# A two-block network on one core: the MLP norms' statistics earlier, one projection's weight split without GpSimd, the last root on ScalarE

## The chip, the cores and the metric

The kernel runs on one core of a Trainium2 chip (trn2). The metric is the device time of one execution in microseconds; lower is better. The median of three runs before the change is 824.85 us.

## The reference

Input is one sequence of 256 tokens with 1024 features; everything is float32. Three residual layers follow one another: a convolution and attention mixer with an MLP (layer 0), a gated recurrence with an MLP (layer 1), and a last block with two attentions over the tokens and a context (block 2).

```python
def rmsnorm(x, g):
    y = x * rsqrt(mean(x * x, -1) + 1e-6)
    return y * g

def first_block(x, ...):
    x = x + mixer_ab(rmsnorm(x, mix_norm[0]), ...)                    # layer 0
    x = x + square(relu(rmsnorm(x, mlp_norm[0]) @ w_up[0])) @ w_down[0]
    u = rmsnorm(x, mix_norm[1]) @ c_w_in                              # layer 1
    gate, xr = split(u, 2)
    y = rg_lru(causal_depthwise_conv(xr, conv_w) + conv_b) * gelu(gate)
    x = x + y @ c_w_out                                               # "layer 1's projection"
    x = x + square(relu(rmsnorm(x, mlp_norm[1]) @ w_up[1])) @ w_down[1]
    return rmsnorm(x, final_norm)

# second_block: h = rmsnorm(x)*(1+scale)+shift, hc the same of the context; MLA and neighborhood
# attention, two gated output products, y @ w_out, residual, and a last rmsnorm
```

## The kernel before

**Layout.** Activations are transposed: 128 features on the partitions, 8 feature blocks of 256 tokens. A matmul multiplies a 128x128 weight block by 256 columns. To keep float32 precision each operand is split into a high and a low part, and each product takes three matmuls (`mm3`, lines 383 to 385): high x high, high weight x low input, low weight x high input. The weights arrive as 240 units of 512 KB in the order of use, by DMA into a ring of 4 buffers (`raw`). `prep` (lines 321 to 326) makes of a unit `wh` (a rounding copy, line 323 on ScalarE) and `wl` (raw minus `wh`, line 326 on VectorE or GpSimd); POLICY names the engines for each unit, as "ag": copy by ScalarE and subtraction by GpSimd, "av": ScalarE and VectorE. The ring of `wh` and `wl` holds 6 units, 12 while `wx` is open, and 14 in a part of it. `more(n)` prepares n units ahead; `unit` takes the next.

**Order.** A list scheduler gives each engine its order when the program is built, from the order in the code and from what is ready in its own model of time; on the chip each engine keeps that order and waits on semaphores. `inorder(engines)` chains what is traced inside it on the named engines in the order of the code; `issue_after(i)` queues instructions behind i on i's own engine alone.

**Statistics.** `ssq` (line 437) squares x on ScalarE in four pieces (line 442) and adds them on GpSimd (lines 444 and 445), into a tile `ssum` of which there is one for each pool. `csum` (line 452) sums over partitions with tiny matmuls into PSUM, `meaneps` (line 458) makes mean + eps on VectorE, `rsq` (line 463) raises to -0.5 on GpSimd, `across` (line 470) broadcasts over partitions with four matmuls, and `spread` (line 476) copies that to SBUF on ScalarE.

**The MLP** (`mlp`, line 972 on). Each of 16 pairs p does `up(p)`, two units of 24 matmuls, then relu and square (`mr`, `mah` on ScalarE, `ma` on GpSimd, `mal` on VectorE); from p = 2 on, two units of the down product follow (`krow`, 24 matmuls each). The norm's factor is applied to the sum at the end: since relu and square are homogeneous, the factor is 1/(mean + eps), the tile `R2`, first read in `proj_tail`. `ssq` stands behind up(4), csum, meaneps and a reciprocal of 128x2 behind up(6), spread behind up(8). `unit` also calls one small background task (`tick`): in MLP 0 the modulation products on VectorE, in MLP 1 the context's statistics (`ctx_setup`). These use the same tile `ssum`: their ssq is the task of the 9th unit, their csum that of the 14th (the second of up(4)), their spread that of the 15th.

**Layer 1's projection** (end of `layer1`). PE and ScalarE are chained in the code's order here. `root(1)` takes a square root on ScalarE and runs four scans on VectorE; `gelu`; `done(p)` multiplies on VectorE and splits the product (ScalarE copy, VectorE subtraction) into the projection's inputs 2p and 2p+1; `wrow(k)` multiplies input k by weight unit `wo1` k. Units 0 to 3 of `wo1` are "ag". The last three rows are in `proj_tail`.

**The end** (`b2_out`). Squares of the result are summed by `stat` (line 1580); meaneps, rsq on GpSimd and across give the last factor; five VectorE multiplications (line 1614) each start a DMA to the output.

Of the kernel before, what the change touches and what calls it, by code (L numbers as in the profile page):

```python
# [11 lines left out]
F32 = mybir.dt.float32  # L12
# [35 lines left out]
POLICY["wo1"] = ("ag",) * 4 + ("av",) * 4  # L48
# [201 lines left out]
class Kern:  # L250
# [183 lines left out]
    def lo(self, l, src, h):  # L434
        self.nc.vector.tensor_tensor(l, src, h.bitcast(F32), op=ALU.subtract)  # L435
# [49 lines left out]
    def run(self):  # L485
# [13 lines left out]
        with self.pool("xp") as xp:  # L499
# [9 lines left out]
            self.pad(cp, 32)  # L509
# [339 lines left out]
    def proj_tail(self, acc, name, ins, gname, g0, xs, R2=None, mp=None, sums=(), after=None):  # L849
# [8 lines left out]
        for b in range(4):  # L858
# [17 lines left out]
            if xs is not None:  # L876
                for k in ks:
                    V.scalar_tensor_tensor(xs[1][:, k], x[:, k], g[k % 2], xs[0][:, k].bitcast(F32),  # L878
                                           op0=ALU.mult, op1=ALU.subtract)
# [91 lines left out]
    def mlp(self, mp, l):  # L971
# [22 lines left out]
        for p in range(16):  # L994
            if l == 0 and p >= 9:
                if p == 9:
                    self.pad(self.cp, 96)
                    self.hs = [self.t(self.cp, [128, 2112], f"hc{c}", F32R) for c in "hl"]
                    self.pad(self.cp, 160)
                self.ahead = min(2 * p - 14, 13)  # L1000
            if l == 1 and p == 4:
                self.wx, self.slot = None, 0
            up(p)
            if p == 4:
                parts = self.ssq(mp, x)
            if p == 6:
                v = self.meaneps(self.csum(parts), D)
                rv = self.t(self.cp, [128, 2], "rv")
                V.reciprocal(rv, v)
            if p == 8:  # L1010
                R2 = self.spread(mp, rv, "R2")
            if p >= 2:
                for k in (2 * p - 4, 2 * p - 3):
                    self.krow(acc, self.unit("down"), A.pop(k), k == 0, False)
# [8 lines left out]
    def layer1(self, lp):  # L1023
# [101 lines left out]
        with self.inorder(*PIN):  # L1125
# [39 lines left out]
            for k in range(4):  # L1165
                if k == 2:
                    done(2)
                if k == 3:
                    done(3)
                wrow(k)  # L1170
                self.more(1 if k == 0 else 2)
# [93 lines left out]
    def b2_kv(self, bp, ep, d):  # L1265
# [96 lines left out]
        zpair("za", 1, ep, cqn)  # L1362
        d.update(kb=kb, vb=vb, krh=krh, krl=krl, ck=ck, wk=wk, va=va, bp=bp)
# [10 lines left out]
    def b2_attn(self, bp, ap, d):  # L1374
# [117 lines left out]
        def gdone(nm, p):  # L1492
            def f(ps):
                tg[nm, p] = self.t(bp, [128, 512], f"t{nm}", bufs=2)
                S.activation(tg[nm, p], ps, AF.Tanh, scale=0.5)
            return f
# [45 lines left out]
    def b2_out(self, op, d):  # L1542
# [11 lines left out]
        for p in range(4):  # L1554
            if p > 1:
                d["gpair"]("ga", p)
                d["gpair"]("gb", p)
                d["oproj"]("oa", p)
            d["oproj"]("ob", p)
            y = tg["ga", p]  # L1560
            V.tensor_tensor(y, y, tg["gb", p], op=ALU.add)
            self.split(self.pair(y), ys[0][:, 2 * p:2 * p + 2], ys[1][:, 2 * p:2 * p + 2])
            if p == 1:
                R1 = self.spread(op, d["r1"], "R1")
                for k in range(8):
                    V.scalar_tensor_tensor(x[:, k], x[:, k], self.p("fin", k), R1, op0=ALU.mult, op1=ALU.mult)
        def orow(w, k, ms, end):
            for m in ms:
                o = last[:, :T] if m == 7 else acc[m // 2][:, (m % 2) * T:(m % 2 + 1) * T]
                c = slice(m * 128, m * 128 + 128)  # L1570
                self.mm3(o, (w[0][:, c], w[1][:, c]), yrow(k), k == 0 and (m % 2 == 0 or m == 7), end)
        for k in range(6):
            orow(self.unit("wo2"), k, range(8), False)
# [8 lines left out]
        def scale(b):  # L1582
            for k in (2 * b, 2 * b + 1):
                S.activation(x[:, k], x[:, k], AF.Copy, scale=self.p("fg2", k))
# [18 lines left out]
        with self.tc.issue_after(si.ins):  # L1603
            for b in range(1, 4):
                scale(b)
# [5 lines left out]
        RF = self.across(self.rsq(self.meaneps(st[:, :2], D)))  # L1611
# [25 lines left out]
```

## Time and profile before

| | us |
|---|---|
| runs: median (lowest to highest) | 824.85 (819.03 to 830.13) |
| the profiled execution | 821.14 |
| its span, first to last instruction | 819.4 |
| PE (TensorE matmuls) busy | 787.9 (96%) |
| DVE (VectorE) busy | 576.4 (70%) |
| ACT (ScalarE) busy | 473.2 (58%) |
| POOL (GpSimd) busy | 199.0 (24%) |

The profiled execution lies 3.71 us under the median. All times in the views are from the start of the span. PE counts as busy while any matmul is in its pipeline, so a stretch without idle time can still differ in how many matmuls start in it; the windows view gives that number behind an x. PEclk is the granted clock as a share of 2.4 GHz. A line such as L326 is that of the helper which issued the instruction.

### The profile page before, as it was taken

What the parts mean: (1) busy time and instruction counts of PE and PEld (TensorE: products, weight loads), DVE (VectorE), ACT (ScalarE), POOL (GpSimd) and SP (SyncE); (2) the same over time, 40 slices, a digit from 0 to 9 for tenths busy, and PEclk for the clock granted to TensorE, in tenths of its full rate; (3) what the DMA queues carried; (4) which work ended last, traced back from release to release, by engine and by line L of the source; (5) the groups of instructions that cost most, each with busy time, mean ns of one, the idle gap of its engine ahead of it and who ended that gap; (6) DMA issues with size and microseconds to landing.
All of it is one profiled execution on the core that took longest, in us unless ns stands there. A gap on an engine that the chain in (4) does not pass through costs nothing.

```text
span 819.4 us, 16154 instructions
## 1 busy us (share of the span) xinstructions
PE 787.9 (96%) x6480; PEld 756.0 (92%) x6480; DVE 576.4 (70%) x952; ACT 473.2 (58%) x739; POOL 199.0 (24%) x151
## 2 busy tenths in 40 slices
PE   6999989999999999979999999999999999999996
PEld 5997889999999999978999999999989988889996
DVE  6999669999989787578746545557634877565843
ACT  5568656455545657877745444445626587765533
POOL 4796643011101202330531110111000022320001
PEclk9999999999999999999999999999999999999997
DMA  7874357787988832238726656664335533555531
GB/s 239 292 222 130 103 181 247 292 311 272 322 307 283 286 113 88 62 124 302 239 99 210 193 189 190 197 196 164 94 119 151 159 105 102 176 163 176 185 101 52
DMA packets 41259, 152.32 MB, mean 186 GB/s; under 512 B 4576, under 2 KB 5088, under 8 KB 39008
## 3 DMA queue, kind: packets, MB, share of 16 engines
q1 hardware_dynamic: 40752, 149.19, 55.5%
q10 hardware_dynamic: 432, 2.10, 0.7%
q8 instruction: 51, 0.84, 0.4%
q14 instruction: 24, 0.20, 0.1%
HBM read 149.17 MB, written 2.10 MB: 185 GB/s over the span
## 4 chain that ended last, share of the span: by engine, by line
PE 59%; issue 19%; DVE 8%; ACT 8%; POOL 4%; DMA 2%; SPq 0%; POOLq 0%; DVEq 0%; ACTq 0%
PE mm L383 10%; PE mm L384 10%; PE mm L385 10%; PE acc L384 7%; PE acc L383 7%; PE acc L385 7%; POOL ma L989 3%; PE acc L1423 2%; PE acc L1451 2%; PE mm L1460 2%; ACT wh L323 1%; DMA raw<-in_wst 1%; DVE wl L326 1%; PE mm L470 1%; DMA x<-in_xT 1%
## 5 line engine op out<-in xcount | busy, mean ns | idle before, releaser
L323 ACT ACTIVATE wh<-raw 128x1024 fp32r<-128x1024 f32 (+1 forms) x190 | 198.3, 1048 | 162.5 <-PE mm L384 64.2
L326 DVE TENSOR_TENSOR wl<-raw,wh 128x1024 fp32r<-128x1024 f32 (+1 forms) x159 | 197.6, 1250 | 100.1 <-ACT wh L323 98.3
L383 PE MATMUL mm<-xsh,wh 128*128 128x256 f32 x752 | 210.4, 280 | 0.0
L384 PE MATMUL mm<-xsl,wh 128*128 128x256 f32 x752 | 209.1, 278 | 0.0
L385 PE MATMUL mm<-xsh,wl 128*128 128x256 f32 x752 | 209.1, 278 | 0.0
L383 PEld LDWEIGHTS mm<-xsh,wh 128*128 128x128 f32 x752 | 141.7, 188 | 3.7 <-issue 3.3
L384 PEld LDWEIGHTS mm<-xsl,wh 128*128 128x128 f32 x752 | 141.7, 188 | 0.6 <-DVE xsl L878 0.2
L385 PEld LDWEIGHTS mm<-xsh,wl 128*128 128x128 f32 x752 | 141.3, 188 | 0.0
L989 POOL TENSOR_TENSOR ma<-mr 128x512 f32<-128x512 f32 x32 | 49.5, 1548 | 246.2 <-ACT mr L987 246.2
L384 PE MATMUL acc<-mal,wh 128*128 128x256 f32 x360 | 100.1, 278 | 1.0 <-DVE mal L435 1.0
L383 PE MATMUL acc<-mah,wh 128*128 128x256 f32 x360 | 100.3, 279 | 0.0
L385 PE MATMUL acc<-mah,wl 128*128 128x256 f32 x360 | 100.0, 278 | 0.0
L326 POOL TENSOR_TENSOR wl<-raw,wh 128x1024 fp32r<-128x1024 f32 x31 | 74.2, 2414 | 43.8 <-ACT wh L323 43.8
L323 ACT ACTIVATE wxh<-raw 128x1024 fp32r<-128x1024 f32 x47 | 49.2, 1055 | 38.8 <-DMA raw<-in_wst 34.9
L384 PEld LDWEIGHTS acc<-mal,wh 128*128 128x128 f32 x360 | 67.9, 189 | 1.2 <-DVE mal L435 1.2
L383 PEld LDWEIGHTS acc<-mah,wh 128*128 128x128 f32 x360 | 67.7, 188 | 0.0
L385 PEld LDWEIGHTS acc<-mah,wl 128*128 128x128 f32 x360 | 67.6, 188 | 0.0
L326 DVE TENSOR_TENSOR wxl<-raw,wxh 128x1024 fp32r<-128x1024 f32 x44 | 56.6, 1299 | 8.0 <-ACT wxh L323 8.0
L384 PE MATMUL mm<-xsl,wxh 128*128 128x256 f32 x208 | 58.1, 279 | 0.6 <-DVE xsl L878 0.6
L383 PE MATMUL mm<-xsh,wxh 128*128 128x256 f32 x208 | 58.3, 280 | 0.0
L385 PE MATMUL mm<-xsh,wxl 128*128 128x256 f32 x208 | 58.0, 279 | 0.0
L915 DVE CUSTOM_DVE_ANT_0 mdump<-mw,cv 128x1024 f32<-128x1024 f32 x40 | 48.7, 1217 | 2.7 <-DMA mw<-in_modw 2.6
(386 smaller groups left out, 1855.9 us busy)
## 6 DMA issues: line engine op xcount, KB each, us to landing
raw<-in_wst SPq DMA_DIRECT2D x240, 512.0 KB, 4.1
mw<-in_modw SPq DMA_DIRECT2D x12, 1024.0 KB, 7.2
nb<-in_nab SPq DMA_DIRECT2D x16, 256.0 KB, 3.7
ab<-in_alibi ACTq DMA_DIRECT2D x1, 1536.0 KB, 8.9
x<-in_xT SPq DMA_DIRECT2D x4, 256.0 KB, 4.9
cv<-in_cvec SPq DMA_DIRECT2D x1, 1024.0 KB, 4.7
cx<-in_cT SPq DMA_DIRECT2D x1, 1024.0 KB, 7.3
xd<-x SPq DMA_DIRECT2D x1, 1024.0 KB, 4.6
```

What stands on the lines that cost most here:

```text
L323: nc.scalar.activation(wh, r, AF.Copy)
L326: (nc.vector if lo == "v" else nc.gpsimd).tensor_tensor(wl, r, wh.bitcast(F32), op=ALU.subtract)
L383: mm(out, w[0], x[0], start=start, stop=False, skip_group_check=True)
L384: mm(out, w[0], x[1], start=False, stop=False, skip_group_check=True)
L385: return mm(out, w[1], x[0], start=False, stop=stop, skip_group_check=True)
L470: self.lasts = self.nc.tensor.matmul(ps[:, j * 128:(j + 1) * 128], rc[:, j:j + 1].to_broadcast([128, 128]), self.ident, start=True, stop=True)
L915: V.tensor_tensor_reduce(d, w, cv[:, s * 1024:(s + 1) * 1024], 0.5, 0.0, op0=ALU.mult, op1=ALU.add, accum_out=self.mod[:, s * 24 + i:s * 2 ...
L989: G.tensor_tensor(a, r, r, op=ALU.mult)
L1423: PE.matmul(sc[i], Q[tag, h][a][:, qs], K[tag, h][b], start=a + b == 0, stop=a == 1)
L1451: PE.transpose(pt[:, i * 128:(i + 1) * 128], P[:, i * 128:(i + 1) * 128], self.ident)
L1460: PE.matmul(o[64 * hh:64 * hh + 64, :T], vt[:, i, h * 64:h * 64 + 64], PTs[tag, h][:, i], start=i == 0, stop=i == 3, skip_group_check=True)
```

## The change

Five edits. (1) The policy of `wo1`: units 0 to 2 are copied and subtracted by VectorE, 3 to 7 by ScalarE and VectorE. (2) In layer 1's projection done(2) and done(3) stand behind rows 0 and 1, and the weights prepared there are queued on VectorE behind the subtraction of that done. (3) In each MLP ssq is at p = 1; in p = 4, with PE in the code's order, csum comes ahead of up(4) and ScalarE makes mean + eps from PSUM; ahead of the second down unit of that pair come across and a VectorE reciprocal of the whole 128x256 tile, from PSUM. (4) The spread of `R1` goes from `b2_out` to the end of the za step in `b2_kv`. (5) At the end ScalarE takes the square root (a dummy Sqrt stands behind the last Tanh), VectorE a reciprocal of 128x2, and two thirds of the scaling copies go behind the root.

```diff
-POLICY["wo1"] = ("ag",) * 4 + ("av",) * 4
+POLICY["wo1"] = ("vv",) * 3 + ("av",) * 5
@@ mlp, loop over p
-            up(p)
-            if p == 4:
-                parts = self.ssq(mp, x)
-            if p == 6:
-                v = self.meaneps(self.csum(parts), D)
-                rv = self.t(self.cp, [128, 2], "rv")
-                V.reciprocal(rv, v)
-            if p == 8:
-                R2 = self.spread(mp, rv, "R2")
-            if p >= 2:
-                for k in (2 * p - 4, 2 * p - 3):
+            with self.inorder(PE.engine) if p == 4 else nullcontext():
+                if p == 4:
+                    v = self.t(self.cp, [128, 2], "rv")
+                    S.activation(v, self.csum(parts), AF.Identity, scale=1.0 / D, bias=self.eps)
+                up(p)
+                if p == 1:
+                    with self.tc.issue_after(self.lastxl.ins):
+                        parts = self.ssq(mp, x)
+                for k in (2 * p - 4, 2 * p - 3) if p >= 2 else ():
+                    if k == 5:
+                        R2 = self.t(mp, [128, T], "R2")
+                        V.reciprocal(R2, self.across(v))
                     self.krow(acc, self.unit("down"), A.pop(k), k == 0, False)
@@ layer1
-            for k in range(4):
-                if k == 2:
-                    done(2)
-                if k == 3:
-                    done(3)
+            wrow(0)
+            done(2)
+            with self.tc.issue_after(self.lastlo.ins):
+                self.more(1)
+            wrow(1)
+            done(3)
+            with self.tc.issue_after(self.lastlo.ins):
+                self.more(2)
+            for k in (2, 3):
                 wrow(k)
-                self.more(1 if k == 0 else 2)
+                self.more(2)
             wrow(4)
@@ b2_kv, behind zpair("za", 1, ...)
+        d["R1"] = self.spread(bp, d["r1"], "R1")
@@ b2_out
-                R1 = self.spread(op, d["r1"], "R1")
@@
+        with self.tc.issue_after(self.lastt.ins):
+            S.activation(self.warm, self.warm, AF.Sqrt)
@@
-            for b in range(1, 4):
-                scale(b)
+            sc = scale(1)
 ... (the five stat calls)
-        RF = self.across(self.rsq(self.meaneps(st[:, :2], D)))
+        sd = self.t(op, [128, 2], "sd")
+        with self.tc.issue_after(sc.ins):
+            sd_ = S.activation(sd, st[:, :2], AF.Sqrt, scale=1.0 / D, bias=self.eps)
+        with self.tc.issue_after(sd_.ins):
+            scale(2)
+            scale(3)
+        V.reciprocal(sd, sd)
+        RF = self.across(sd)
```

## Rows read from the trace of the kernel before

**Rows 1.** The page, part 1: busy us, share of span, instructions; PE.

```profile
PE 787.9 (96%) x6480; PEld 756.0 (92%) x6480; DVE 576.4 (70%) x952; ACT 473.2 (58%) x739; POOL 199.0 (24%) x151
```

**Rows 2.** Windows: stretch, length, busy (count) PE PEld DVE ACT POOL, PEclk, DMA, GB/s.

```profile
340.00:360.00 20.00, 16.47 (x127) 15.78 (x125) 12.39 (x18) 18.46 (x25) 7.15 (x4) 0.91 0.17 55
360.00:380.00 20.00, 17.28 (x142) 16.67 (x143) 16.95 (x17) 10.85 (x14) 2.81 (x1) 1.00 0.78 260
```

**Rows 3.** Timeline of PE, 348 to 385: start, us, instruction, count [idle before <-releaser].

```profile
354.26 0.58 PE L385 MATMUL acc<-xr,wl 128*128 128x256 f32 x1 [1.47 <-POOL wl L326]
360.05 0.39 PE L385 MATMUL acc<-xr,wl 128*128 128x256 f32 x1 [1.45 <-POOL wl L326]
367.42 0.39 PE L384 MATMUL acc<-ysl,wh 128*128 128x256 f32 x1 [1.57 <-DVE ysl L435]
...
372.60 0.39 PE L384 MATMUL acc<-ysl,wxh 128*128 128x256 f32 x1 [0.94 <-DVE ysl L435]
```

**Rows 4.** Timeline of POOL, 300 to 385: units 1, 2 and 3.

```profile
351.85 2.36 POOL L326 TENSOR_TENSOR wl<-raw,wh 128x1024 fp32r<-128x1024 f32 x1 [5.75 <-ACT wh L323]
357.62 5.19 POOL L326 TENSOR_TENSOR wl<-raw,wh 128x1024 fp32r<-128x1024 f32 x2 [3.42 <-ACT wh L323]
```

**Rows 5.** Timeline of DVE, 341 to 385: done(0) and (1), root(1), done(2) and (3).

```profile
341.25 1.47 DVE L1119 TENSOR_TENSOR th<-th,gl 128x512 f32<-128x512 f32 x2
...
354.17 1.29 DVE L1106 TENSOR_TENSOR ig<-ig,th 128x512 f32<-128x512 f32 x2 [2.65 <-ACT th L1103]
...
357.73 5.63 DVE L1119 TENSOR_TENSOR th<-th,gl 128x512 f32<-128x512 f32 x2
363.28 1.21 DVE L326 TENSOR_TENSOR wl<-raw,wh 128x1024 fp32r<-128x1024 f32 x1
```

**Rows 6.** Windows, columns as in rows 2: behind the first wait, and in MLP 0.

```profile
354.40:357.80 3.40, 3.40 (x19) 3.40 (x20) 3.40 (x7) 3.39 (x5) 0.18 (x1) 0.59 0.45 154
160.00:175.00 15.00, 15.00 (x130) 15.00 (x129) 14.79 (x29) 9.17 (x11) 1.91 (x2) 1.00 0.83 318
205.00:220.00 15.00, 15.00 (x135) 15.00 (x134) 14.58 (x19) 8.49 (x10) 1.84 (x1) 1.00 0.93 309
```

**Rows 7.** Timeline of ACT, 341 to 375: unit 1's copy, a table load.

```profile
350.73 1.04 ACT L323 ACTIVATE wh<-raw 128x1024 fp32r<-128x1024 f32 x1
...
354.15 1.28 ACT L1115 ACT_TABLE_LOAD   x1
```

**Rows 8.** Groups of DVE by form: line, operation, form, count | busy us, mean ns.

```profile
L1326 DVE CAST wkh<-wh 128x512 fp32r<-128x512 f32 x1 | 0.4, 421 | 0.0
...
L1009 DVE RECIPROCAL rv<-var 128x2 f32<-128x2 f32 x2 | 0.3, 160 | 0.0
...
L938 DVE RECIPROCAL sm<-sm 128x8 f32<-128x8 f32 x1 | 0.2, 196 | 0.0
```

**Rows 9.** Lines 444 and 470: ns min/median/max, first and last start.

```profile
L444 POOL TENSOR_TENSOR ssum<-ssum,sqt x9: 1283/1294/2382, 119.0 to 421.9; 128x512 f32<-128x512 f32 x9
...
L470 PE MATMUL mm<-ident,rv x8: 272/275/276, 198.9 to 466.6; 128*128 128x128 f32 x8
```

**Rows 10.** Timeline of ACT in MLP 0, 143 to 166.

```profile
161.94 1.06 ACT L323 ACTIVATE wxh<-raw 128x1024 fp32r<-128x1024 f32 x1 [5.05 <-DMA raw<-in_wst]
```

**Rows 11.** Timelines of ACT and POOL in MLP 1: ssq of x.

```profile
418.28 0.63 ACT L442 ACTIVATE ssum<-x 128x512 f32<-128x512 f32 x1 [6.77 <-PE mm L452]
...
419.20 4.02 POOL L444 TENSOR_TENSOR ssum<-ssum,sqt 128x512 f32<-128x512 f32 x3
423.30 0.81 POOL L445 TENSOR_TENSOR ssum<-ssum 128x256 f32<-128x256 f32 x1
```

**Rows 12.** Timeline of the end, 810 to 819.

```profile
811.32 0.71 POOL L463 TENSOR_TENSOR rc<-var,mhalf 128x2 f32<-128x2 f32 x1 [2.69 <-DVE var L458]
...
812.08 1.22 PE L470 MATMUL mm<-ident,rc 128*128 128x128 f32 x4 [1.04 <-POOL rc L463]
```

**Rows 13.** Line 936, ACT's smallest: ns min/median/max, start, form.

```profile
L936 ACT ACTIVATE sm<-sm x1: 208/208/208, 137.9 to 137.9; 128x8 f32<-128x8 f32 x1
```

More of the change, by code (lines that the diff above doesn't have):

```diff
@@ L434, in lo @@
     def lo(self, l, src, h):
-        self.nc.vector.tensor_tensor(l, src, h.bitcast(F32), op=ALU.subtract)
+        self.lastlo = self.nc.vector.tensor_tensor(l, src, h.bitcast(F32), op=ALU.subtract)
     def ssq(self, pool, x3):
@@ L508, in run @@
             G.memset(self.mhalf, -0.5)
-            self.pad(cp, 32)
+            self.eps = self.t(cp, [128, 1], "eps")
+            G.memset(self.eps, EPS)
             with self.pool("l0") as lp:
@@ L877, in proj_tail @@
                 for k in ks:
-                    V.scalar_tensor_tensor(xs[1][:, k], x[:, k], g[k % 2], xs[0][:, k].bitcast(F32),
-                                           op0=ALU.mult, op1=ALU.subtract)
+                    self.lastxl = V.scalar_tensor_tensor(xs[1][:, k], x[:, k], g[k % 2], xs[0][:, k].bitcast(F32),
+                                                         op0=ALU.mult, op1=ALU.subtract)
             self.more(max(0, min(1 + b, 3) - len(self.q)))
@@ L1494, in f @@
                 tg[nm, p] = self.t(bp, [128, 512], f"t{nm}", bufs=2)
-                S.activation(tg[nm, p], ps, AF.Tanh, scale=0.5)
+                self.lastt = S.activation(tg[nm, p], ps, AF.Tanh, scale=0.5)
             return f
@@ L1563, in b2_out @@
             if p == 1:
-                R1 = self.spread(op, d["r1"], "R1")
                 for k in range(8):
-                    V.scalar_tensor_tensor(x[:, k], x[:, k], self.p("fin", k), R1, op0=ALU.mult, op1=ALU.mult)
+                    V.scalar_tensor_tensor(x[:, k], x[:, k], self.p("fin", k), d["R1"], op0=ALU.mult, op1=ALU.mult)
         def orow(w, k, ms, end):
@@ L1583, in scale @@
             for k in (2 * b, 2 * b + 1):
-                S.activation(x[:, k], x[:, k], AF.Copy, scale=self.p("fg2", k))
+                i = S.activation(x[:, k], x[:, k], AF.Copy, scale=self.p("fg2", k))
+            return i
         def fold(b):
```

## The prediction

> **What bounds the kernel now.** I read the page's busy times first: PE is busy 787.9 of 819.4 us [rows 1], and the order of its matmuls follows the code, so only three things can save time: PE's idle stretches (31.5 us in all), a lower granted clock, and a wider spacing of matmuls while PE counts as busy. Next I read the windows of 20 us. Through most of the two MLPs PE has no idle time; the stretch with layer 1's projection is the worst in the middle of the kernel: 16.47 and 17.28 us busy of 20 [rows 2]. Then I read the timeline of PE there: four waits, two for the low halves of weights that POOL makes and two for the low halves of the projection's inputs that DVE makes, 1.47 + 1.45 + 1.57 + 0.94 = 5.43 us [rows 3]. The timelines of POOL, DVE and ACT say why, and the windows of MLP 0 show the spacing.
>
> **Layer 1's projection (edits 1 and 2).** POOL's subtraction takes 2.36 us for unit 1 and 5.19 us for units 2 and 3 [rows 4], DVE's 1.21 [rows 5]. Unit 1 is ready at 351.85 + 2.36 = 354.21, and PE goes on at 354.26; unit 2 is the second wait. The third wait has the same origin by a detour. While POOL works on units 2 and 3 (357.62 to 362.81), done(2) and done(3)'s two multiplications take 5.63 us on DVE; the same pair took 1.47 us at 341.25, with POOL idle [rows 5]. That is 4.2 us by which everything on DVE behind them is late, the low half of input 4 among it. And ACT copies units 0 and 1 (about 1.04 us each [rows 7]) ahead of the root and of gelu in a queue kept in the code's order; DVE stands 2.65 us idle for that root [rows 5].
>
> Edit 1 takes all four POOL jobs away, and ACT's copies of units 0 to 2. DVE gets three copies and four subtractions. A copy of 128x1024 isn't in the trace; half that size takes 0.42 us [rows 8], so it lies between 0.42 and 0.84, and I take 0.7. That is 3 x 0.7 + 4 x 1.21 = 6.9 us more for DVE. Its cover is 20 - 12.39 = 7.6 us of idle time between 340 and 360 [rows 2] and the 4.2 us that come free. If that cover were gone, each vector-made unit would hold root(1)'s scans and the products behind them for 1.9 us. The waits on POOL go in full (2.92), the third and fourth (2.51) go as far as DVE gets to the inputs sooner: about 2.1 us for the two copies off ACT's queue, 4.2 us for the undisturbed products. Also the clock: in the stretch behind the first wait PE's granted clock averages 0.59, so most of it is at 1.2 GHz, and 19 matmuls start in 3.4 us where 135 x 3.4 / 15 = 31 would at 2.4 GHz [rows 6]; 12 x 0.111 = 1.3 us. What is late next is unit 3, still copied by ACT behind gelu: gelu ends 2.1 us sooner, near 354.5 (the load at 354.15 takes 1.28 [rows 7], the two gelus about 0.6 each, less 2.1), then copy 1.04 and subtraction 1.21, ready near 357. PE wanted unit 1 at 354.26 - 1.47 = 352.8 and would want unit 3 two rows of 24 matmuls, 5.4 us, later: just in time. I leave 1.2 us of new waiting for that and for the last three units, which ACT and DVE make behind done(3). A unit made sooner also frees its buffer sooner, so SP issues a later unit's DMA sooner; its order stays. Sum: -5.43 - 1.3 + 1.2 = **-5.5 us**; bounds: -7.4 (nothing left, and one short wait ahead of these gone too) and -2 (DVE as the new bound).
>
> **The MLP norms (edit 3).** The squares and sums cost nothing new: the scheduler had the sums on POOL from 119.0 on in MLP 0 [rows 9], though they stand behind up(4) in the code. The issue_after there binds DVE only, and ssq has no DVE instruction, so it holds nothing. On DVE a mean and a reciprocal of 128x2 (0.16 each) give way to a reciprocal of 128x256. From 2 to 8 columns a reciprocal grows from 160 to 196 ns [rows 8], 6 ns a column; so 0.16 + 254 x 0.006 = 1.7 us, between 0.4 (one column a cycle as other operations run) and that with a third added. PE pays nothing as long as weights are ready ahead: between 160 and 175 DVE is 14.79 of 15 us busy and PE has no idle time [rows 6]. Without that lead it would be 1.7 us in MLP 0. In MLP 1 DVE is far from full.
>
> Three consequences lie on PE itself. First, **the spacing**. With the clock at 1.00 in both, 130 matmuls start in 160:175 and 135 in 205:220 [rows 6]; the step lies at the broadcast of the norm (198.9 [rows 9]), and I saw steps at such interruptions only. What makes them the trace does not show. Edit 3 moves that broadcast from behind up(8) to the middle of pair 4's down product, 3.75 pairs of 96 matmuls at 0.115 us, or 41 us earlier. If the closer spacing again starts there, 41 x 5/135 = **-1.5 us**. Bounds: -2.6 if the 70 us ahead of 198.9 have it, +3.0 if the wide one lasts the 80 us (7.5 pairs) from there to the end of MLP 0.
>
> Second, **a wait for ScalarE in MLP 0**. PE is chained, so the broadcast, now near 157, waits for ScalarE's mean, and behind it the rest of the pair waits too. ACT's queue there stands still from 156.9 to 161.94 for a weight DMA [rows 10]. The mean itself waits for csum, with weight copies and the relu of pair 4 queued behind it on ACT. It is traced half a pair ahead of that relu, so I judge its place to be ahead of the stop and take 0; behind the stop it would be 162 + 1.3 - 157 = 6 us.
>
> Third, **the context's statistics in MLP 1**. They share the one tile `ssum`. Before, x's squares waited 6.77 us for the context's csum [rows 11]; now the context's wait for x's csum, ahead of up(4), while the context's own csum is traced between the two units of up(4). From the first square to the last sum takes 424.11 - 418.28 = 5.8 us [rows 11]; 24 matmuls cover 2.7. The scheduler can fill the remaining 3.1 us with up(5), whose weights and PSUM are free. I take **+0.5**; bounds 0 and 3.1 + 1.3 for a clock that falls.
>
> **The end (edits 4 and 5).** Edit 4 moves four matmuls and a copy into another stretch of products: 0, and 0.5 us at most if PE waited for the factor there. Today PE stands 1.04 us between the last sum and the broadcast, of which GpSimd's power is 0.71 [rows 12]. Now a root (0.21 by ACT's smallest row [rows 13]; at most the 0.71 it replaces) and a reciprocal of 0.16 with three hand-overs of 0.05: 0.5. So **-0.5**, bounds -0.6 and 0. The copies put behind the root (4 x 0.4) end before the multiplications that need them. The table for Sqrt is loaded behind the last Tanh, 1.28 us by the row of a load [rows 7], where ACT has nothing PE waits for.
>
> The Trainium skill (ScalarE: Activation LUTs, section What ACT_TABLE_LOAD costs) speaks against a root here: about 2.66 us for every switch to another set, half of it a drain. The trace has 1.28 us for a load and shows no drain as a row. By the page the end would be 2.1 us longer instead of 0.5 shorter if the load fell there; by the row 0.8 longer.
>
> **Sum.** -5.5 - 1.5 + 0.5 - 0.5 = -7.0 us against the profiled execution's 821.14: 814.1. That execution lies 3.71 us under the median of the runs; on the median the sum is 817.9, and I forecast **818**.
>
> **The rivals.**
> A, DVE is the new bound: the projection's waits move to DVE's longer list and only 2 us are won there. For it: DVE was 16.95 of 20 us busy behind the projection [rows 2] and gets 6.9 us more. Against it: the 4.2 us that come back. Time: 818 + 3.5 = 821.5.
> B, the other side, the spacing: the added broadcasts leave PE in the wide spacing, in MLP 0 to its end (+3.0 instead of -1.5) and in MLP 1 from pair 4 on, 12 pairs or 130 us x 5/135 = +4.8. Time: 818 + 4.5 + 4.8 = 827.3, slower than before. It decides once the wide spacing covers 190 us more than today (7.0 x 135/5). For it: steps occur without a visible rule; against it: at the broadcast in MLP 0 the step went the good way.
> C, pair 4's chain: ACT's mean comes behind the stopped weight copy, 6 us and 1.3 for the clock: 825; or MLP 1's 4.4 us instead of 0.5: 822. For it: ACT's stop is real and five microseconds long; against it: the mean's place by the code.
> D, the table load falls into the end all the same, say because the dummy root's set is not kept: 1.3 us by the row, 819.3. For it speaks no row; against it, the weight copy of rows 7 runs behind another set's function and has no load of its own, so copies and squares behind the dummy root should need none.
>
> **Chances.** Forecast 0.50, A 0.18, B 0.12, C 0.14, D 0.03, anything else 0.03. Runs of one kernel spread from 819 to 830, so about 2% is what a measurement of this kernel tells from no change. The forecast's own range is 812 to 823. With A and C it reaches to 827; the low end is the bounds' best sum (-10.6) less half the spread of the runs: 809. B's upper part stays out. Over 2% faster is below 808.4: 0.04. Over 2% slower is above 841.3, B and C together and more: 0.02. Within: 0.94.
>
> **What would show it.** Right: no POOL instruction on L326 between 340 and 365; done(2) and (3)'s products near 0.7 us each; PE's waits there below 2 us in all and the clock at 1.00; the first matmul of MLP 1 about 6 us sooner; broadcast to last multiplication 0.5 us sooner. Wrong: a PE wait on ACT's mean near 157 or on csum in MLP 1's pair 4; windows in the MLPs with 130 starts where there were 135; DVE subtractions that PE waits for behind the projection.

## The result, and the profile after

The changed kernel takes 827.88 us (median of 20 runs, 821.94 to 836.25), the kernel before 822.55 beside it (20 runs, 818.49 to 830.13). The ratio is 1.0063, 95% interval 1.0046 to 1.0081: 0.5 to 0.8% slower, less than 2%, and above the predicted range of 809 to 827. The profiled execution took 829.03 us with a span of 827.2, 7.9 us more than the one before; the medians differ by 5.3. Part of the 7.9 belongs to that one execution: PE is 1.7 us late from 63.69 on and 2.9 us late where MLP 0 begins, behind layer 0's mixer, which no edit touches.

Where the rest lies is told by the start of the same matmul in both traces, with those of csum and broadcast left out of the count. The changed kernel is late by 2.9 us where the trace of before stands at 124 us, by 5.3 at 309, 6.9 at 334, 1.6 at 400, 8.7 at 561 and 8.6 at 810. So MLP 0 cost 2.4 us and layer 1 ahead of its projection 1.6; the projection with the start of MLP 1 gave 5.3; the rest of MLP 1 cost 7.2, and the end gave 0.8.

Busy times of the page, to be held against [rows 1]: PE is busy 3.9 us longer for the same 6480 matmuls.

```profile
PE 791.8 (96%) x6480; PEld 759.8 (92%) x6480; DVE 586.5 (71%) x957; ACT 472.0 (57%) x739; POOL 189.9 (23%) x147
```

**Layer 1's projection** went as forecast in this trace. Windows of the changed kernel, columns as in [rows 2]:

```profile
340.00:360.00 20.00, 19.53 (x167) 19.33 (x166) 16.16 (x21) 15.35 (x21) 3.43 (x1) 1.00 0.29 107
360.00:380.00 20.00, 18.99 (x168) 18.80 (x167) 17.18 (x22) 14.15 (x18) 0.00 (x0) 1.00 0.54 178
```

In these 40 us 335 matmuls start instead of 269 [rows 2], 66 x 0.115 = 7.6 us of work more ahead of MLP 1's start, and the granted clock stays at 1.00. Of the four waits of [rows 3] two new ones are left, and a longer one than before stands where MLP 1 begins. Timeline of PE, 356 to 386, with the rows of ACT ahead of the last:

```profile
358.73 0.39 PE L383 MATMUL acc<-xr,wh 128*128 128x256 f32 x1 [0.47 <-DVE th L1101]
366.38 0.39 PE L385 MATMUL acc<-xr,wl 128*128 128x256 f32 x1 [1.01 <-DVE wl L326]
384.88 0.39 PE L383 MATMUL mm<-xsh,wxh 128*128 128x256 f32 x1 [1.57 <-ACT xsh L873]
...
383.37 1.06 ACT L323 ACTIVATE wh<-raw 128x1024 fp32r<-128x1024 f32 x1 [0.53 <-DMA raw<-in_wst]
384.33 0.89 ACT L873 ACTIVATE xsh<-x,par 128x256 fp32r<-128x256 f32 x2
```

The last of them takes back a part of the gain: ACT makes MLP 1's first inputs (`xsh`) behind a weight copy that waited for its DMA.

**MLP 1** lost what was won and more. PE, POOL and ACT around the context's statistics, from their timelines:

```profile
422.57 0.61 PE L452 MATMUL mm<-ones,ssum 128*128 128x1 f32 x4 [2.65 <-POOL ssum L445]
425.86 0.60 PE L470 MATMUL mm<-ident,rc 128*128 128x128 f32 x4
429.13 0.60 PE L470 MATMUL mm<-ident,rv 128*128 128x128 f32 x4
...
417.02 0.63 ACT L442 ACTIVATE ssum<-cx 128x512 f32<-128x512 f32 x1 [2.37 <-PE mm L452]
417.73 3.99 POOL L444 TENSOR_TENSOR ssum<-ssum,sqt 128x512 f32<-128x512 f32 x3 [2.07 <-ACT ssum L442]
421.80 0.72 POOL L445 TENSOR_TENSOR ssum<-ssum 128x256 f32<-128x256 f32 x1
```

The context's squares start when x's csum has freed the tile, and PE waits 2.65 us for their sum. Behind the two broadcasts the matmuls start farther apart, to the end of MLP 1. Windows of 15 us of the changed kernel in MLP 0 and MLP 1, then MLP 1 at 470 in the kernel before (135 starts) and in the changed one (130):

```profile
205.00:220.00 15.00, 15.00 (x134) 15.00 (x134) 15.00 (x19) 8.19 (x9) 1.50 (x1) 1.00 0.88 297
510.00:525.00 15.00, 15.00 (x130) 15.00 (x129) 7.66 (x7) 6.42 (x7) 1.59 (x1) 1.00 0.65 190
...
470.00:485.00 15.00, 15.00 (x135) 15.00 (x134) 7.79 (x8) 7.05 (x8) 1.60 (x1) 1.00 0.55 187
...
470.00:485.00 15.00, 15.00 (x130) 15.00 (x129) 7.34 (x7) 7.25 (x10) 1.60 (x2) 1.00 0.64 189
```

By the starts of three successive matmuls there are just two spacings at full clock, 340 and 353 ns for three, "close" and "wide" from here on. The changed kernel is wide from 426 to 568; the kernel before was wide only from 444 to 466 of that stretch. 142 - 22 = 120 us x 5/135 is 4.4 us; with the wait of 2.65 that is 7.05 of the 7.2 us that MLP 1 cost.

**The end of MLP 0** lost 4.0 us, more than the 1.5 that MLP 0 had gained until then: the changed kernel is 1.4 us late where before stands at 279, and 5.4 at 293. The last relu stands on ACT behind a copy that waits for its weight's DMA, and the half clock follows. Timelines of ACT and PE:

```profile
283.24 1.06 ACT L323 ACTIVATE wh<-raw 128x1024 fp32r<-128x1024 f32 x1 [1.28 <-DMA raw<-in_wst]
284.21 0.58 ACT L988 ACTIVATE mr<-mm 128x512 f32<-128x512 f32 x1
...
286.25 1.06 ACT L323 ACTIVATE wh<-raw 128x1024 fp32r<-128x1024 f32 x1 [0.81 <-DMA raw<-in_wst]
...
285.50 0.38 PE L383 MATMUL acc<-mah,wxh 128*128 128x256 f32 x1 [1.59 <-ACT mah L989]
287.24 0.38 PE L384 MATMUL acc<-mal,wxh 128*128 128x256 f32 x1 [1.35 <-DVE mal L435]
```

The window behind these waits, with a granted clock of 0.53:

```profile
288.00:291.50 3.50, 3.50 (x19) 3.50 (x19) 2.25 (x4) 0.84 (x3) 0.00 (x0) 0.53 0.73 256
```

**The kernel's end** gained 0.8 us. ACT's root, DVE's reciprocal and the broadcast:

```profile
819.69 0.26 ACT L1621 ACTIVATE sd<-mm,eps 128x2 f32<-128x2 f32 x1 [0.39 <-PE mm L1588]
...
819.99 0.17 DVE L1625 RECIPROCAL sd<-sd 128x2 f32<-128x2 f32 x1 [1.60 <-ACT sd L1621]
...
820.30 0.85 PE L470 MATMUL mm<-ident,sd 128*128 128x128 f32 x4 [0.65 <-DVE sd L1625]
```

The wait is 0.65 us instead of 1.04 [rows 12], and the broadcast takes 0.85 instead of 1.22.

**Layer 1 ahead of the projection** lost 1.6 us: PE waits 1.29 us for `xch` instead of 0.89, and the granted clock behind it is 0.72 from 334.0 to 338.5. Six of the nine traces here of kernels with edit 3 in MLP 0 lose 1.4 to 1.8 us at this place, none of the eight others more than 0.3. What ties it to edit 3 is open.

### The profile page after: what moved, and what is told of

Same layout as the page of the kernel before. It is cut to its first block, busy times and chain, and to the rows that moved or that the text cites. A ratio compares the mean times of both kernels' runs of the same rounds, so it can differ in the third digit from the quotient of the medians.

```text
span 827.2 us, 16144 instructions
## 1 busy us (share of the span) xinstructions
PE 791.8 (96%) x6480; PEld 759.8 (92%) x6480; DVE 586.5 (71%) x957; ACT 472.0 (57%) x739; POOL 189.9 (23%) x147
## 4 chain that ended last, share of the span: by engine, by line
PE 56%; issue 18%; DVE 10%; ACT 7%; POOL 4%; DMA 4%; SPq 0%; DVEq 0%; POOLq 0%; ACTq 0%
PE mm L383 10%; PE mm L384 9%; PE mm L385 9%; PE acc L384 7%; PE acc L383 7%; PE acc L385 7%; DMA raw<-in_wst 4%; POOL ma L990 3%; PE acc L1430 2%; PE acc L1458 2%; PE mm L1467 2%; DVE wl L326 1%; ACT wh L323 1%; POOL wl L326 1%; DVE mm L613 1%
## 5 line engine op out<-in xcount | busy, mean ns | idle before, releaser
L323 ACT ACTIVATE wh<-raw 128x1024 fp32r<-128x1024 f32 (+1 forms) x187 | 195.4, 1048 | 167.0 <-PE mm L384 64.8
L326 DVE TENSOR_TENSOR wl<-raw,wh 128x1024 fp32r<-128x1024 f32 (+1 forms) x163 | 206.4, 1272 | 106.0 <-ACT wh L323 104.8
L326 POOL TENSOR_TENSOR wl<-raw,wh 128x1024 fp32r<-128x1024 f32 x27 | 65.3, 2442 | 31.9 <-ACT wh L323 31.9
L326 DVE TENSOR_TENSOR wxl<-raw,wxh 128x1024 fp32r<-128x1024 f32 x44 | 54.8, 1261 | 5.5 <-ACT wxh L323 5.4
```

The costliest lines, as they stand in the source:

```text
L323: nc.scalar.activation(wh, r, AF.Copy)
L326: (nc.vector if lo == "v" else nc.gpsimd).tensor_tensor(wl, r, wh.bitcast(F32), op=ALU.subtract)
```

## The experiments

The theory after the result: the projection gains; edit 3 loses, by MLP 1's wait and by the wide spacing. The main rival: the projection's new order starves MLP 1 of weights, and that is the loss. Ratios are to the kernel before, measured beside each kernel, with 95% intervals. A trace is of one execution; those of norms_only, own_tile, extra_broadcast, changed_2 and policy_end are of the fastest execution of their kernel, up to 8 us under its median.

### Which edit costs

**end_only**: the kernel before with edits 4 and 5.

```diff
+        d["R1"] = self.spread(bp, d["r1"], "R1")     # b2_kv; away from b2_out
...
-        RF = self.across(self.rsq(self.meaneps(st[:, :2], D)))
...
+            sd_ = S.activation(sd, st[:, :2], AF.Sqrt, scale=1.0 / D, bias=self.eps)
```

> The kernel before with edits 4 and 5 alone (spread of R1 moved, root on ScalarE at the end). Theory: the wait ahead of the last broadcast falls from 1.04 to 0.65 us and nothing else changes: 0.3 to 0.7 us faster, ratio 0.999. Rival (the moved spread or the dummy root disturbs the za step or the gates): 0.5 us slower or more.

0.9994 (0.9973 to 1.0014). In its trace the wait ahead of the broadcast is 0.65 us. The ratio alone can't tell 0.5 us from nothing.

**proj_only**: the kernel before with edits 1 and 2.

```diff
+POLICY["wo1"] = ("vv",) * 3 + ("av",) * 5
...
+            done(2)                                  # behind wrow(0)
+            with self.tc.issue_after(self.lastlo.ins):
```

> The kernel before with edits 1 and 2 alone (layer 1's projection). Theory (the loss comes from the MLP norms): the stretch of the projection gives 5 to 8 us, of which part is paid back where MLP 1 begins, because weight units come later there; MLP 1 keeps the spacing of before (close from the context's broadcast near 421 on) and has no wait for csum. So 3 to 5 us faster than before, ratio 0.994 to 0.997. Rival (the projection's new order starves MLP 1 of weights and that is the loss): no faster than before or up to 3 us slower.

0.9983 (0.9962 to 1.0004), 1.4 us. Less than the theory's 3 to 5, and not the rival's loss. Its trace has the projection's gain and, like that of the changed kernel, a wait for `xsh` at MLP 1's start, 1.47 us.

**norms_only**: the kernel before with edit 3.

```diff
+                    S.activation(v, self.csum(parts), AF.Identity, scale=1.0 / D, bias=self.eps)
...
+                    if k == 5:
...
+                        V.reciprocal(R2, self.across(v))
```

> The kernel before with edit 3 alone (the MLP norms). Theory: in MLP 0 the closer spacing gains about 2 us, and PE then catches up with the weights and waits there for up to 4 us; in MLP 1 a wait of 2 to 3 us for the context's csum, and the spacing of 117.8 ns from there to the end of MLP 1, 4.5 us. Together 5 to 9 us slower, ratio 1.006 to 1.011. Rival (edit 3 is neutral, the loss lies in edits 1 and 2): within 2 us of before.

1.0174 (1.0135 to 1.0213), more than expected; the profiled execution, with 827.13 us the fastest of the six, is 6.0 us above that of before. The wait for csum is there to the hundredth (2.65 us at 423.09), and here the clock falls behind it; the spacing behind the broadcasts is close. A window behind the wait:

```profile
423.50:427.00 3.50, 3.50 (x22) 3.50 (x22) 0.16 (x1) 0.00 (x0) 0.71 (x1) 0.66 0.02 5
```

The slower executions have a lower granted clock, 0.983 to 0.986 over the whole span where the profiled one has 0.989. By an estimate, the lost share times the span, that is 2.5 to 5 of the 5 to 11 us that they take longer; what adds the rest, no trace shows.

**mlp1_old**: the changed kernel, with edit 3 in MLP 0 alone.

```diff
-            with self.inorder(PE.engine) if p == 4 else nullcontext():
-                if p == 4:
+            new = l == 0        # the p == 4, 6, 8 lines of before serve l == 1
+            with self.inorder(PE.engine) if new and p == 4 else nullcontext():
+                if new and p == 4:
```

> The changed kernel, with MLP 1's norm as before (squares at pair 4, csum at pair 6, spread at pair 8) and MLP 0's as changed. Theory: MLP 1's wait for csum (2.66 us) goes, and the spacing becomes close again at the context's broadcast (4.5 us): 5 to 7 us less than the changed kernel, which is 1 us on either side of the kernel before (ratio 0.998 to 1.001). Rival (MLP 1's loss has another cause, for instance the late weights): as slow as the changed kernel, ratio 1.005 to 1.007.

0.9982 (0.9963 to 1.0001): against the changed kernel's 1.0063 that is 6.7 us less. So the loss lies in MLP 1's norm, and the rival falls. The parts aren't independent, though: proj_only, norms_only and end_only add up to +1.51%, and the kernel with all five edits is 0.63% slower. Why edit 3 alone costs more than the whole is open.

### The wait, and a second trace

**own_tile**: the changed kernel, the context's sum in a tile of its own.

```diff
-        s = self.t(pool, [128, 2, T], "ssum")
+        s = self.t(pool, [128, 2, T], tag)      # "ssumc" for the context
```

> The changed kernel, with a tile of its own for the context's sum of squares in MLP 1, so that it waits for nothing of x's. Theory: PE's wait of 2.65 us ahead of the context's csum in pair 4 goes. If the wide spacing behind it (426 to 568 in the changed kernel's trace) came from that stall, it goes too: 5 to 7 us less than the changed kernel, ratio 0.998 to 1.001. If it comes from the two broadcasts that stand one row of 24 matmuls apart, it stays in some executions: 2.5 to 4 us less than the changed kernel, ratio 1.001 to 1.003. Rival (the csum wait costs nothing in the end, since weights would be late there anyway): as the changed kernel, 1.005 to 1.007.

1.0065 (1.0042 to 1.0087): no gain. The wait for csum is gone, and the spacing is wide all the same from 426.8 to 564.6, so it comes without the stall too. And a new wait has come. POOL, then PE:

```profile
391.87 5.80 POOL L444 TENSOR_TENSOR ssumc<-ssumc,sqt 128x512 f32<-128x512 f32 x3
...
399.30 1.50 POOL L990 TENSOR_TENSOR ma<-mr 128x512 f32<-128x512 f32 x1
...
399.96 0.39 PE L384 MATMUL acc<-mal,wh 128*128 128x256 f32 x1 [2.11 <-DVE mal L435]
```

Free of the tile, the context's sums go ahead of the MLP's own product `ma` on GpSimd: 2.11 us lost for 2.65 won.

**changed_2**: the changed kernel without any edit, for a second trace.

> The changed kernel once more, for another trace of it beside the others. Theory: the wait of 2.65 us ahead of the context's csum in MLP 1 is there again, since it is in the order; the broadcast in MLP 0 waits for ScalarE's mean or comes just behind it, and the spacing behind the broadcasts is wide in MLP 0, in MLP 1 or in both: 143 us of wide spacing in MLP 0 or 140 in MLP 1 cost 5.5 us each. Ratio 1.004 to 1.009. Rival (the wide spacing in MLP 1 was that one execution's): close behind both broadcasts, and the time of such an execution near 823.

1.0066 (1.0040 to 1.0092). The wait (2.66 us) and the wide spacing in MLP 1 (421.6 to 562.6) are there again; MLP 0 is close behind its broadcast, as in the first trace.

### The spacing

**extra_broadcast**: one more broadcast in MLP 1.

```diff
                 up(p)
+                if l == 1 and p == 6:
+                    self.across(v)
```

> The changed kernel, with one more broadcast of four matmuls behind up(6) in MLP 1, whose result nobody reads. It costs 0.4 us of PE. Theory (a broadcast that PE meets in the wide spacing lets it go on in the close one, as at 198.9, 421.0 and 466.3 in the kernel before): if the spacing behind pair 4 is wide, 353 ns for three matmuls, it is 340 from the extra broadcast on, near 450, and the kernel takes up to 3.5 us less than the changed one. Rival (the spacing is set by something else): no change of the spacing at the extra broadcast, and 0.4 us more.

The spacing turns at the very instruction. Windows on either side of it (447.22):

```profile
428.00:446.00 18.00, 18.00 (x155) 18.00 (x154) 14.84 (x21) 10.23 (x15) 1.59 (x1) 1.00 0.54 156
449.00:467.00 18.00, 18.00 (x161) 18.00 (x161) 9.27 (x9) 8.21 (x10) 3.12 (x2) 1.00 0.61 190
```

The profiled execution is the fastest of four (822.91 us), but the ratio is 1.0115 (1.0084 to 1.0147): in time the theory fails, the kernel is slower than the changed one. No trace shows what the slower executions do. One reason could be that the same instruction turns a close spacing wide, as in the next run.

**before_extra**: the kernel before, one more broadcast behind up(9) in MLP 1.

```diff
+            if l == 1 and p == 9:
+                self.across(rv)
```

> The kernel before with one more broadcast of four matmuls in MLP 1 behind up(9), whose result nobody reads. Theory (a broadcast met in the close spacing leaves the wide one): wide from there, near 478, to the end of MLP 1, 3.5 us slower with the 0.4 us of the matmuls themselves, ratio 1.003 to 1.006. Rival (the spacing follows from stalls and not from the broadcasts): 0.4 us slower, ratio 1.000 to 1.001, spacing unchanged.

1.0052 (1.0023 to 1.0080), 4.3 us slower (1.9 to 6.6) by four matmuls. Windows on either side of them (477.11):

```profile
467.00:476.00 9.00, 9.00 (x82) 9.00 (x81) 4.74 (x5) 4.37 (x6) 1.60 (x1) 1.00 0.63 185
479.00:488.00 9.00, 9.00 (x79) 9.00 (x78) 4.44 (x5) 3.58 (x4) 1.41 (x1) 1.00 0.61 178
```

It is wide from there to 570, the end of MLP 1, and 92 us x 5/135 is 3.4. Over all traces here, between 125 and 570 us, a broadcast of four matmuls that PE met without waiting turned the close spacing wide 13 times of 13, and the wide close 53 times of 59. A csum of four turned close wide 43 times of 43 and left wide as it was 25 times of 27. So csum, broadcast, csum, broadcast (before) should end close, and in MLP 1 it does in 12 traces of 12 (in before_extra up to the added one). Csum, csum, broadcast, broadcast (edit 3) should end wide, and does in four of the five traces that have it. But only own_tile gets there by the counted turns, wide, wide, close, wide. In the changed kernel, changed_2 and extra_broadcast the second broadcast, 3.2 us behind the first, met the wide spacing and left it wide: three of the six exceptions. That the order goes with the wide spacing is shown; whether it acts by these turns or by the closeness of the two broadcasts is not.

**ctx_later**: the changed kernel, the context's tasks behind x's.

```diff
-        self.bg += [lambda: None] * 8 + [stats] + ...
+        self.bg += [lambda: None] * 16 + [stats] + ...
```

> The changed kernel, with the context's statistics in MLP 1 eight background tasks later, behind x's: csum and broadcast of x, then csum and broadcast of the context. Theory: the context's squares find the tile free, so there is no csum wait (2.65 us) and none on GpSimd's products (2.1 us with a tile of its own); and csum, broadcast, csum, broadcast leaves the close spacing behind the last one, where csum, csum, broadcast, broadcast left the wide one. 5 to 7 us less than the changed kernel, ratio 0.998 to 1.001. Rival (the wide spacing follows from edit 3's place in the middle of a pair): 2 to 3 us less, ratio 1.002 to 1.004.

0.9961 (0.9939 to 0.9983): 8.4 us less than the changed kernel, more than expected. No wait for csum, and close from 445 to the end of MLP 1; one edit took away both, so the split between them rests on the traces; the same window as above:

```profile
510.00:525.00 15.00, 15.00 (x135) 15.00 (x134) 7.19 (x8) 8.44 (x10) 3.20 (x2) 1.00 0.63 190
```

### Edit 1 and edit 2

**policy_only** has the first line alone, **order_only** the others.

```diff
+POLICY["wo1"] = ("vv",) * 3 + ("av",) * 5
...
+            done(2)                                  # layer1, as in the change
+            with self.tc.issue_after(self.lastlo.ins):
+                self.more(1)
```

> The kernel before with edit 1 alone: units 0 to 2 of layer 1's projection by VectorE, 3 to 7 by ScalarE and VectorE. Theory (the waits there come from GpSimd and from what it does to VectorE): both waits on GpSimd go, the waits on the inputs shrink; 2 to 4 us less in the stretch 350 to 380, and no late weights at the start of MLP 1, so 1.5 to 3 us faster over all. Rival (the order of edit 2 is needed): VectorE makes later units ahead of the products, waits on the inputs grow, 0 to 2 us slower.

> The kernel before with edit 2 alone: done(2) and done(3) behind rows 0 and 1, later units' preparation behind their subtractions. Theory: the waits on GpSimd stay, done(2) and done(3) still run beside GpSimd, and the later weights come later: 0 to 3 us slower than before, with waits at the start of MLP 1 of 2 us or more. Rival (edit 2 is what wins the time): 2 to 4 us faster.

policy_only 0.9965 (0.9936 to 0.9994), order_only 0.9983 (0.9963 to 1.0003). Edit 1 wins by itself; order_only fits neither forecast. Each of the eight traces with edit 2 has a wait of 1.18 to 1.65 us for `xsh` where MLP 1 begins (1.57 in the rows above); none of the nine without edit 2 has. So the wait comes with edit 2. What edit 2 takes away is about as large: policy_only waits 1.03 and 0.72 us for low halves of the projection's inputs, proj_only for none. By the start of the same matmul, from 334 to 400 us, edit 1 without edit 2 gives 5.0 to 5.8 us in five traces, both together 3.2 to 5.5 in six (own_tile, with its new wait, left out), and the four other traces without edit 1 are 0.5 to 1.2 us ahead of before. The rows above give the next link: ACT makes `xsh` behind a weight copy that waited for its DMA. How edit 2 delays these weights, by queueing the preparation of later units behind done(2) and done(3), fits its order but is argued, not shown: the DMA share between 360 and 380 us doesn't separate the kernels, 0.70 in policy_only and in the second trace of the changed kernel alike. The first of these windows:

```profile
360.00:380.00 20.00, 17.23 (x145) 16.51 (x144) 17.73 (x22) 13.38 (x18) 0.00 (x0) 1.00 0.70 237
```

### MLP 0, and the best version

**policy_end**: the kernel before with edits 1, 4 and 5; **policy_end_2** is the same kernel beside the changed one.

```diff
+POLICY["wo1"] = ("vv",) * 3 + ("av",) * 5
...
+            sd_ = S.activation(sd, st[:, :2], AF.Sqrt, scale=1.0 / D, bias=self.eps)
```

> The kernel before with edits 1, 4 and 5: the policy of wo1 and the end, without the new order in the projection and without the norms. Theory: the gains add, 3.2 us of edit 1 (ratio 0.9965) and 0.4 us of the end: ratio 0.995 to 0.997. Rival (edit 1's result came by the chance of a few executions): ratio 0.998 to 1.000.

> Edits 1, 4 and 5 alone, once more beside the changed kernel. Theory (edit 3 costs the changed kernel some 9 us in its two MLPs, edit 2 one or two more): ratio 0.990 to 0.995 to the kernel before. Rival (the first result of this kernel was helped by few executions): 0.996 to 0.999.

0.9911 (0.9880 to 0.9943) and 0.9898 (0.9869 to 0.9928): the fastest kernel of the study, 815.94 and 817.07 us. More than the sum of policy_only and end_only (0.4%), at the edge of what the intervals allow the first time and beyond it the second; why is open. In the first trace both MLPs are close behind their last broadcasts.

**no_edit2**: the changed kernel with the projection's order of before and the context's tasks later.

```diff
-            wrow(0)
-            done(2)
+            for k in range(4):                       # layer1, as before the change
...
-        self.bg += [lambda: None] * 8 + [stats] + ...
+        self.bg += [lambda: None] * 16 + [stats] + ...
```

> The changed kernel with the context's statistics later and without edit 2. Theory: as the kernel with edits 1, 4 and 5, with MLP 0's norm broadcast 41 us earlier, which saves up to 1.5 us of wide spacing there where the weights allow it: ratio 0.993 to 0.997. Rival (MLP 0's norm costs as much as it gives, since PE catches up with its weights): ratio 0.996 to 0.999.

0.9951 (0.9927 to 0.9974), in the theory's range, but 0.4% behind policy_end beside it: by that edit 3 in the MLPs costs some 3.3 us even with MLP 1 mended (the two intervals overlap). The trace says where it may lie. In MLP 0 the broadcast waits for ACT's mean, which stands behind a stopped weight copy; the timelines of ACT and PE of ctx_later, where it is the same:

```profile
155.38 1.06 ACT L323 ACTIVATE wh<-raw 128x1024 fp32r<-128x1024 f32 x1 [2.84 <-DMA raw<-in_wst]
156.35 0.24 ACT L1007 ACTIVATE rv<-mm,eps 128x2 f32<-128x2 f32 x1
...
156.64 0.71 PE L470 MATMUL mm<-ident,rv 128*128 128x128 f32 x4 [0.78 <-ACT rv L1007]
```

The window of ctx_later in MLP 0:

```profile
205.00:220.00 15.00, 15.00 (x130) 15.00 (x129) 14.83 (x17) 8.44 (x9) 1.43 (x1) 1.00 0.82 277
```

MLP 0 stays wide to its end, 145 us x 5/135 = 5.4 against a close spacing all the way. Against the kernel before it lost 2.5 us between 124 and 309: its PE has no wait at the end of MLP 0, where that of the changed kernel waits 2.94. Of eight traces with this broadcast in pair 4 four wait (0.32 to 0.78 us), and three of these and one of the others stay wide behind it. At its old place behind up(8) it left close in eight of eight. In MLP 0, from 124 to 309 us, the nine traces with edit 3 take 1.6 us longer than the one of before on average (-0.3 to +3.0), the eight with the old place 1.0 less (-2.8 to +1.1).

**broadcast_later**: no_edit2 with the broadcast one pair later.

```diff
-                    if k == 5:
+                    if k == 7:
```

> The changed kernel without edit 2, the context's statistics later, and the broadcast of each MLP's norm one pair later (ahead of the second down unit of pair 5). Theory (in MLP 0 the broadcast waits for ScalarE's mean, which stands behind a weight copy that waits for its DMA, and PE goes on in the wide spacing afterwards): ScalarE's mean is ready about 11 us before the broadcast, no wait there, and the close spacing from near 170 to the end of MLP 0; 2 to 4 us less than the same kernel with the broadcast in pair 4 (ratio 0.9951), so 0.990 to 0.994. Rival (the wide spacing in MLP 0 has nothing to do with the wait): ratio 0.994 to 0.997, spacing in MLP 0 still wide behind the broadcast.

0.9925 (0.9896 to 0.9955), as the theory says; no wait, and close from the broadcast at 171.54 on:

```profile
175.00:190.00 15.00, 15.00 (x134) 15.00 (x134) 14.96 (x19) 8.08 (x9) 1.36 (x1) 1.00 0.80 294
```

From 246 on it is wide again, without a broadcast near, behind a matmul that started 300 ns after the one before instead of 113: a very short wait turns the pace too. The interval overlaps that of no_edit2; the mechanism is seen in one trace, its price not fixed by the times.

**The account** in ratios: edits 1, 4 and 5 -0.89%; edit 3 with the context's tasks later +0.40% (no_edit2 against policy_end); edit 2 +0.10% (ctx_later against no_edit2, inside the intervals); the order of the statistics in MLP 1 +1.02% (the changed kernel against ctx_later). The sum is the measured +0.63%, as it must be for a chain of differences; what it tells is the size of the links, each of them good to 0.3 or 0.4%.

## Why the prediction was wrong, step by step

- **What bounds the kernel**: right. PE's waits, its clock and its spacing made every difference that a trace shows.
- **The projection, -5.5 us**: right in mechanism, and in size by the two traces of the changed kernel: from 334 to 400 us, MLP 1's start included, the same matmul gains 5.3 and 5.5 us. The runs give less, 1.4 us for proj_only and 2.9 for policy_only, each good to some 2 us. And the gain is edit 1's; what edit 2 gave or cost lies inside the intervals. DVE's copies of 128x1024 take 683 ns (forecast 700), the two products 1.27 us instead of 5.63 [rows 5]. Three details failed. GpSimd is not out of the stretch: a subtraction of another unit stands at 340.79 and takes 3.43 us, beside two of DVE's that take 4.57. Timelines of POOL and DVE:

```profile
340.79 3.43 POOL L326 TENSOR_TENSOR wl<-raw,wh 128x1024 fp32r<-128x1024 f32 x1 [4.95 <-ACT wh L323]
...
340.74 4.57 DVE L326 TENSOR_TENSOR wl<-raw,wh 128x1024 fp32r<-128x1024 f32 x2
```

  Undisturbed the three take 2.36 [rows 4] and 2 x 1.21 us [rows 5], 4.78 one after the other; together they need 4.57. The Trainium skill (SBUF — State Buffer, section SBUF: two separate sides) calls the port that VectorE and GpSimd share an exclusive lock and no split of bandwidth; by that rule the two take turns, and the rows agree. The 1.2 us left for new waiting behind the projection came out at 2.7: 1.48 us of waits in it and 1.77 at MLP 1's start, against 0.55 there before. And the step "a unit made sooner also frees its buffer sooner" fits the traces with edit 1 and without edit 2, which have no wait where MLP 1 begins; with edit 2 PE waits there again.
- **MLP 0's spacing, -1.5 us**: the close spacing did start at the broadcast in the two traces of the changed kernel, but MLP 0 came out 2.4 us longer in the first and 0.3 shorter in the second. In the first, PE waited for late weights and gave 4.0 us back at the end of MLP 0. I had asked what hides DVE's reciprocal, and not what the faster PE will run into. The premise was a matter of luck too: the wide stretch ahead of 198.9 that the edit was to shorten is there from 130 on in the trace of before, but four of the eight traces with MLP 0's old order are close until the csum near 175 and wide for 22 us only. And the bound of +3.0 was short: MLP 0 goes on for about 100 us behind 198.9, not 80.
- **ACT's mean in MLP 0, 0 us**: the place on ACT's queue was judged by the code. In the first trace it stood behind a copy that waited 1.26 us for its DMA and came 1.5 us ahead of the broadcast; in four of eight traces it came 0.3 to 0.8 us too late. Rival C named the queue, but priced the wait at 6 us; three of those four traces then stay wide, which C did not name.
- **DVE's reciprocal of 128x256, 1.7 us, covered**: right, 1743 ns, and PE waits for neither of the two. The row of line 1015 (ns min/median/max, first and last start):

```profile
L1015 DVE RECIPROCAL R<-mm x2: 1743/1743/1743, 168.8 to 430.6; 128x256 f32<-128x256 f32 x2
```

- **The context's statistics, +0.5 us, and nothing for MLP 1's spacing**: the step that failed. I let the scheduler fill the wait with up(5). But pair 4 is traced with PE in the code's order, and the task that holds the context's csum is traced inside it, so by the code it was pinned: 2.65 us in each of the four traces with this order and one tile. That is still inside the bounds I gave (0 to 4.4). The sum had no term at all for the spacing in MLP 1: I treated the spacing as MLP 0's alone and left MLP 1 to rival B with a chance of 0.12, 4.8 us from pair 4 on. The first trace shows 4.4 us, and MLP 1 cost 7.2 and 6.6 us in the two traces instead of 0.5. Taking edit 3 out of MLP 1 (mlp1_old) gives 6.7 us back, changing the order of the statistics there (ctx_later) 8.4. B was right about the end in MLP 1, but not in its reason: no broadcast was added there, the order changed. The trace of before could have warned me: the csum met close at 443 ended wide, the three broadcasts met wide in the MLPs, the first and the last of them in [rows 9], ended close, and one met close at 301 ended wide. By these turns csum, csum, broadcast, broadcast ends wide. In the changed kernel it came out so by another way: the wait ahead of the second csum left the close spacing, the first broadcast turned it wide, and the second left it wide.
- **Rival B's 827.3 us** lies beside the measured 827.88 by luck. In the first trace MLP 0's 2.4 us came from PE's waits and not from B's wide spacing, and B has no wait for csum. It also stands on a median of three runs, 3.71 us above the profiled execution; with twenty runs the median before is 822.55, 1.4 above it. So B's own loss of 2.4 us is less than half of the 5.3 measured.
- **The end, -0.5 us**: -0.8 in the trace, of which the wait is 0.39, the same in all eleven traces with edit 5 (0.64 to 0.65 us instead of 1.04). The rest is the clock, 0.71 in the broadcast instead of 0.50, and a matter of the execution: in end_only's trace the broadcast takes 1.19 us behind the same short wait. Rival D fell: the table for the dummy Sqrt loads at 791.9, 1283 ns, and its instruction follows at 793.1. The drain that the Trainium skill (ScalarE: Activation LUTs, section What ACT_TABLE_LOAD costs) adds to each switch shows in no row here either: the load starts 5 ns behind the instruction before it, and the next one 11 ns behind the load. The row of line 1579:

```profile
L1579 ACT ACT_TABLE_LOAD  x1: 1283/1283/1283, 791.9 to 791.9; - x1
```

- **Rival A** (DVE as the bound) fell: two short waits, 1.48 us.

## What to carry to other kernels

A step that saves a wait on PE is judged twice: by the wait, and by what PE meets when it comes sooner, here the weights' DMA and copies queued behind it. Before work is moved into a stretch whose order is pinned, look for background tasks traced in the same stretch, and for tiles that they share. Where an engine counts as busy all the time, count how many of its instructions start; small matmuls put into a dense stream can change the pace of everything behind them, so the last one before a long stretch deserves a look at the windows on either side.

## What the runs showed of the hardware

At full granted clock the stream of 128x256 matmuls runs at one of two paces, 340 or 353 ns for three, and keeps it over hundreds of matmuls, until a wait or small matmuls come between; between 125 and 570 us of the 17 traces no change of pace that lasts lies elsewhere. Four matmuls whose result nobody reads cost 4.3 us (0.5%) by turning it. What in TensorE makes the two paces, and why six of 59 broadcasts left the wide one as it was, stays open.
